# A hybrid decoder layer on one core: attention keys copied out of PSUM at once, the query statistic five half chunks behind its fold, softmax heads two half chunks apart

## The chip, the core and the metric

The kernel runs on one core of a Trainium2 chip. The metric is the device time of one execution in microseconds (us). The median of three executions of the kernel before is 1896.22 us (1896.04 to 1896.8). One further execution was recorded by the hardware profiler; its own time was 1896.41 us and its recorded span 1894.2 us. All rows shown below are of that execution.

## The reference

One decoder layer over 256 tokens of width 2048, float32 throughout. Three residual branches follow each other; each is normed on its way in and again on its way out:

```python
h = rms_norm(x, mix_pre_norm);   x = x + rms_norm(hybrid_mixer(h, ...), mix_post_norm)
h = rms_norm(x, xattn_pre_norm); m = rms_norm(mem, mem_norm)
x = x + rms_norm(cross_attention(h, m, wq, wkv, wo), xattn_post_norm)
h = rms_norm(x, ffn_pre_norm);   x = x + rms_norm(conv_glu_ffn(h, ...), ffn_post_norm)
```

The change lies in the second branch, the attention of 256 tokens over 256 memory tokens with 4 heads of 128:

```python
q = (h @ wq);  k, v = split(mem_n @ wkv)
p = softmax(einsum('bshd,bmhd->bhsm', q, k) * 128 ** -0.5)
return einsum('bhsm,bmhd->bshd', p, v) @ wo
```

## The kernel before

**Products.** Every weight matrix is cut into blocks of up to 512 columns, and each block into chunks of 512 KB that hold two slices of 128 rows (two values of `k`). A chunk is loaded by a DMA on SP's queue into one of four `raw` buffers. ACT casts it to `wh` (line 375) and DVE subtracts to get the rest, `wl` (line 396); each has four buffers. The left operand is split in the same way (`mh, ml` for the memory tokens, `qh, ql` for the normed residual), and TensorE (PE) multiplies three pairs: high by high, low by high, high by low. One slice `k` of a block is therefore 12 matmuls, a *half chunk*. Blocks of kind "fm" give outputs with features on partitions, "tm" with tokens on partitions. `acc` has four PSUM buffers and a block takes two, so the block after next cannot begin before somebody has read the block's results out (its *evacuation*).

**Order of work.** The program writes each engine's instructions in one fixed order. The function `run` goes through the blocks, half chunk by half chunk, and at each half chunk calls `side.half()`. That lets side tasks (Python generators: evacuations, norms, softmax) emit their next piece, up to their `yield`, between the products. Evacuations are bulk tasks, which wait for their turn by a budget of DVE and ACT time; a chain task (`chain=1`) emits one piece at every half chunk. `side.need(task)` emits all that is left of a task on the spot. So the place of a `yield` sets how many half chunks of products lie on PE between two pieces of a task.

**The attention's blocks.** The order is: `w_xk` (keys, operand `mh, ml`), two chunks of `w_xv` (values), all eight chunks of `w_xq` (queries, operand `qh, ql`), the other six chunks of `w_xv`, then four blocks of `w_xo`. `w_xk` and `w_xq` use the same two PSUM buffers. Three side works run beside them:

- `kx_evac`: DVE reads the key products out of PSUM into `kT`, scaled by the memory norm; a bulk task.
- `Residual.run`: DVE and ACT scale the mixer's output `z`, add it to the residual `xr`, and split it into `qh, ql`. The squares of `xr` are summed into `stx`. When all is summed, `early_column` folds the two halves of `stx` (DVE), and `column` then sums over partitions with two matmuls into `st`; from `st` come `var` (DVE) and the scale `stx_c` (GpSimd), which the softmax needs.
- `stagger` and `softmax`: per head, scores `xsc` (PE), row maximum `mx` (DVE), exponentials into `spr` (ACT), division (DVE, `psum` then `spr`), four transposes `xpT` (PE), copy to `pT` (ACT). `spr` has two halves that the heads use in turn. At the end `xo` (PE) multiplies the values `xv` by `pT`, and `split` (ACT, DVE) turns that into `oT`, the operand of the `w_xo` blocks.

The instructions of `act`, `dve` and the matmuls of `mm` are issued through helpers, so many rows of the profile carry line 66 (DVE and ACT) or 181 (PE); the tiles' names tell them apart.

Of the kernel before, what the change touches and what calls it, by code (L numbers as in the profile page):

```python
# [139 lines left out]
def layer(tc, d, dbg=None):  # L140
    with ExitStack() as ctx:
        ctx.enter_context(tc.manual_schedule())
        _layer(ctx, tc, tc.nc, d, dbg or (lambda n, t: None))


def _layer(ctx, tc, nc, d, dbg):
# [21 lines left out]
    def C(name, tag, shape=None, dt=F32):  # L168
        return mp.tile(shape or [P, S], dt, tag=tag, bufs=1, name=name)

    def small(name, shape, bufs=2):
        return mp.tile(shape, F32, tag="sm_" + name, bufs=bufs, name=name)
# [4 lines left out]
    def aux(name, shape=None):  # L177
        return pp.tile(shape or [P, 512], F32, tag="aux", bufs=4, name=name)

    def mm(out, lhsT, rhs, start=True, stop=True):  # L180
        pe.matmul(out, lhsT, rhs, start=start, stop=stop, skip_group_check=True)  # L181
# [61 lines left out]
    class Stat:  # L243
# [64 lines left out]

        def early_column(self):
            self.fold()  # L310
            yield
            yield
            self.column()

        def finish(self, n=2):
# [8 lines left out]
    def block(kind, srcs, xs, evac, before=None, cols=512, pool_=None, pre=None, bankwise=False, tail=0):  # L324

        blocks.append(dict(kind=kind, srcs=srcs, xs=xs, evac=evac, before=before, cols=cols,
                           pool=pool_ or acc, pre=pre, task=None, bankwise=bankwise, tail=tail))
        return blocks[-1]
# [103 lines left out]
    def run():  # L432
# [8 lines left out]
        for b, c0, c1 in order:  # L441
            if c0 == 0:
# [4 lines left out]
                n = (b["cols"] // P + 1) // 2 if b["kind"] == "fm" else 2 * (b["cols"] // 512)  # L447
# [57 lines left out]
            if nt:  # L505
# [9 lines left out]
                n = len(steps)  # L515
# [27 lines left out]
                feed.dma(i + 4)  # L543
            if end:
                b["task"] = side.add(b["evac"](banks))
                if b is xq_:
                    side.need(b["task"])
                pend.append(b["task"])

    def W(name, blk):  # L550
        return [d[name][blk, c] for c in range(d[name].shape[1])]
# [958 lines left out]
    for i in range(2):  # L1510
        for cb in range(4 + AHEAD):
            if cb >= AHEAD:
                before = None
                if cb == AHEAD:
                    before = need_hb if i else need_ha
# [15 lines left out]
    for b in range(4):  # L1531
        block("fm", W("w_mo", b), mo_xs, y_evac(b, sty, "z1", "postg"),
              before=load_x if b == 1 else None)
# [3 lines left out]
    mxs = lambda k: (M["mh"][:, k], M["ml"][:, k])  # L1537
# [13 lines left out]
    def qx_evac(ps):  # L1551
        M["qT"] = [T2("qT") for _ in range(2)]
        for g in range(2):
            act.copy(M["qT"][g], ps[g])
        tasks["sm"] = side.add(stagger([softmax(h) for h in range(4)]), chain=1, free=True)
        yield
# [10 lines left out]
    def stagger(gens):  # L1567

        live, left = [], list(gens)
        live.append(left.pop(0))  # L1570
        next(live[0])
        yield
        yield from M["res"].wait(4)
        while live or left:
            if left:
                live.append(left.pop(0))
            for g in list(live):
                try:
                    next(g)
                except StopIteration:  # L1580
                    live.remove(g)
            yield

    def softmax(h):
        qT, kT = M["qT"], M["kT"]
        q = aux("xsc", [P, 2, S])
        for t in range(2):
            mm(q[:, t], qT[h // 2][:, h % 2, t * P:(t + 1) * P], kT[h // 2][:, h % 2])
        mx = small("mx", [P, 2], bufs=4)
        dve.tensor_reduce(mx, q, axis=AX.X, op=ALU.max)  # L1590
        yield
        if h == 0:
            yield from M["res"].wait(4)
            M["spr"] = C("spr", "bg1", [P, 2, 2, S])
            M["sx"] = small("sx", [P, 2, 2], bufs=1)
            for i, sc in enumerate((128 ** -0.5, -128 ** -0.5)):
                dve.tensor_scalar(M["sx"][:, i], stx.rc, sc, None, op0=ALU.mult)
        sx = M["sx"]
        dve.tensor_mul(mx, mx, sx[:, 1])
        pr = M["spr"][:, h % 2]  # L1600
        ps_ = small("psum", [P, 2])
        for t in range(2):
            act.activation(pr[:, t], q[:, t], AF.Exp, scale=sx[:, 0, t:t + 1], bias=mx[:, t:t + 1], accum_out=ps_[:, t:t + 1])
        dve.reciprocal(ps_, ps_)
        for t in range(2):
            dve.tensor_scalar(pr[:, t], pr[:, t], ps_[:, t:t + 1], None, op0=ALU.mult)
        yield
        q = aux("xpT", [P, 2, S])
        for t in range(2):
            for mt in range(2):  # L1610
                pe.transpose(q[:, mt, t * P:(t + 1) * P], pr[:, t, mt * P:(mt + 1) * P], ident)
        if h % 2 == 0:
            M["pTs", h // 2] = C("pT", f"au{h // 2}", [P, 2, 2, S])
        M["pT", h] = M["pTs", h // 2][:, h % 2]
        act.copy(M["pT", h], q)
        yield
# [9 lines left out]
            split(M["oT"][:, 0, h2 * 2:h2 * 2 + 2], M["oT"][:, 1, h2 * 2:h2 * 2 + 2], q)  # L1626
            yield

    block("fm", W("w_xk", 0), mxs, kx_evac, before=start_res1)
    xv = block("tm", W("w_xv", 0), mxs, vx_evac, tail=2)  # L1630
    xq_ = block("fm", W("w_xq", 0), lambda k: M["res"].tile(k), qx_evac)
    st3 = Stat("st3")
# [6 lines left out]
    for b in range(4):  # L1639
        xo3 = block("fm", W("w_xo", b), lambda k: (M["oT"][:, 0, k], M["oT"][:, 1, k]), y_evac(b, st3, "z2", "xpostg"),  # L1640
              before=need_o if b == 0 else None, bankwise=b == 3)
# [67 lines left out]
    for b in range(32):  # L1709
        fu = block("fm", W("w_fu", b), fu_xs(b), fu_evac(b),  # L1710
              before=start_ffn if b == 0 else None, pool_=aux if b == 2 else acc)
# [126 lines left out]
    for n in range(2):  # L1838
        block("tm", W("w_fd", n), ax(n), fd_evac(n), cols=1024, pool_=acc if n else aux,
              tail=4 if n else 0)  # L1840
    run()
    drain_bulk()

# [91 lines left out]
```

## Time and profile before

| | |
|---|---|
| median of three runs | 1896.22 us |
| the profiled execution, its own time | 1896.41 us |
| its span | 1894.2 us |
| PE busy | 1878.4 us, 99% |
| DVE busy | 1297.0 us, 68% |
| ACT busy | 1012.7 us, 53% |
| `w_xk` ends, first chunks of `w_xv` begin | 744.8 us |
| first product of `w_xq` | 752.26 us |
| first scores | 777.68 us |
| first and last group of transposes | 782.96 and 793.21 us |
| `xo` begins | 803.74 us |

A row of a timeline gives the start in us, the duration, the engine, line, operation and tiles, a count where like instructions are merged, and in square brackets how long the engine sat idle before it and whose work ended that.

### The profile page before, as it was taken

To read this page: it belongs to the slowest core of one execution; us is meant where nothing else is said; L and a number is where in the kernel's file an instruction comes from. 1 tells how busy PE (TensorE), PEld (TensorE's weight loads), DVE (VectorE), ACT (ScalarE), POOL (GpSimd) and SP (SyncE) were. 2 spreads that over 40 slices of the span, in tenths; PEclk is the share of its full clock that TensorE was granted. 3 is DMA by queue.
4 is the path that set the end of the run, shared out by engine and by line. 5 is a ranking of instruction groups with operands and counts; after the bars stand their busy time and mean duration, and the time that the engine had idled before them with its cause. 6 is when DMAs were issued, how large, how long until landed. Compare 5 with 4: busy or idle time off the path is not lost.

```text
span 1894.2 us, 36440 instructions
## 1 busy us (share of the span) xinstructions
PE 1878.4 (99%) x15066; PEld 1788.5 (94%) x15066; DVE 1297.0 (68%) x1834; ACT 1012.7 (53%) x1467; POOL 22.4 (1%) x39
## 2 busy tenths in 40 slices
PE   9999999999999999899999999999999999999998
PEld 9999988999999999899999999999999998888886
DVE  7878787565675857677767766667766675556555
ACT  7676435555454645566555444455444455455554
POOL 0100000000000000000000000000000000000000
PEclk9999999999999999999999999999999999999999
DMA  7655554444556755455555555555566556556554
GB/s 267 184 168 182 183 157 149 136 153 157 167 171 210 268 201 179 134 163 186 193 189 190 191 198 193 197 190 190 191 198 196 195 190 219 192 190 198 191 191 142
DMA packets 98199, 352.20 MB, mean 186 GB/s; under 512 B 11057, under 2 KB 11825, under 8 KB 97649
## 3 DMA queue, kind: packets, MB, share of 16 engines
q1 hardware_dynamic: 97168, 348.86, 56.1%
q8 instruction: 118, 1.93, 0.4%
q10 hardware_dynamic: 864, 1.01, 0.2%
q14 instruction: 49, 0.39, 0.1%
HBM read 347.73 MB, written 2.10 MB: 185 GB/s over the span
## 4 chain that ended last, share of the span: by engine, by line
PE 95%; DVE 2%; ACT 1%; issue 1%; DMA 0%; ACTq 0%; DVEq 0%
PE fm L181 67%; PE tm L181 24%; DVE wl L396 1%; PE gram L181 0%; PE Y L181 0%; ACT wh L375 0%; DVE rows L66 0%; PE lv L181 0%; PE num L181 0%; DMA wsm<-in_w_sm_dram 0%; ACT spr L66 0%; PE X L181 0%; PE gramA L181 0%; PE U L181 0%; DVE ql L66 0%
## 5 line engine op out<-in xcount | busy, mean ns | idle before, releaser
L396 DVE TENSOR_TENSOR wl<-raw,wh 128x1024 fp32r<-128x1024 f32 x640 | 780.1, 1224 | 437.9 <-ACT wh L375 435.1
L375 ACT CAST wh<-raw 128x1024 fp32r<-128x1024 f32 x640 | 668.4, 1049 | 530.5 <-PE fm L181 408.6
L181 PE MATMUL fm<-fh,wh 128*128 128x256 f32 x2048 | 567.4, 277 | 1.4 <-ACT fh L66 1.4
L181 PE MATMUL fm<-fh,wl 128*128 128x256 f32 x2048 | 566.5, 277 | 0.0
L181 PE MATMUL fm<-fl,wh 128*128 128x256 f32 x2048 | 566.4, 277 | 0.0
L181 PEld LDWEIGHTS fm<-fh,wh 128*128 128x128 f32 x2048 | 384.9, 188 | 1.5 <-ACT fh L66 1.5
L181 PEld LDWEIGHTS fm<-fh,wl 128*128 128x128 f32 x2048 | 384.9, 188 | 0.0
L181 PEld LDWEIGHTS fm<-fl,wh 128*128 128x128 f32 x2048 | 384.9, 188 | 0.0
L181 PE MATMUL tm<-wh,as 128*128 128x512 f32 x1024 | 315.7, 390 | 0.8 <-DVE as L66 0.8
L181 PE MATMUL fm<-hh,wh 128*128 128x256 f32 x1072 | 301.9, 282 | 0.0
L181 PE MATMUL fm<-hh,wl 128*128 128x256 f32 x1072 | 299.7, 280 | 0.5 <-DVE wl L396 0.5
L181 PE MATMUL fm<-hl,wh 128*128 128x256 f32 x1072 | 299.3, 279 | 0.0
L181 PEld LDWEIGHTS tm<-wh,as 128*128 128x128 f32 x1024 | 192.2, 188 | 41.1 <-DVE as L66 1.1
L181 PEld LDWEIGHTS fm<-hh,wh 128*128 128x128 f32 x1072 | 202.8, 189 | 1.6 <-ACT hh L66 0.3
L181 PEld LDWEIGHTS fm<-hh,wl 128*128 128x128 f32 x1072 | 202.3, 189 | 1.2 <-DVE wl L396 0.9
L181 PEld LDWEIGHTS fm<-hl,wh 128*128 128x128 f32 x1072 | 202.3, 189 | 0.1
L181 PE MATMUL tm<-wl,as 128*128 128x512 f32 x512 | 199.3, 389 | 0.0
L181 PEld LDWEIGHTS tm<-wl,as 128*128 128x128 f32 x512 | 96.1, 188 | 19.9
L66 ACT CAST as<-ac 128x256 fp32r<-128x256 f32 x128 | 45.6, 405 | 110.8 <-PE tm L181 110.8
L66 DVE TENSOR_TENSOR as<-ac,as 128x256 fp32r<-128x256 f32 x128 | 48.6, 422 | 61.6 <-ACT as L66 61.6
L181 PE MATMUL fm<-mgh,wh 128*128 128x256 f32 x256 | 71.4, 279 | 0.0
L181 PE MATMUL fm<-mgl,wh 128*128 128x256 f32 x256 | 71.2, 278 | 0.0
(376 smaller groups left out, 2168.4 us busy)
## 6 DMA issues: line engine op xcount, KB each, us to landing
raw<-in_w_fu_dram SPq DMA_DIRECT2D x256, 512.0 KB, 4.3
raw<-in_w_in_dram SPq DMA_DIRECT2D x160, 512.0 KB, 3.7
raw<-in_w_fd_dram SPq DMA_DIRECT2D x128, 512.0 KB, 4.3
raw<-in_w_br_dram SPq DMA_DIRECT2D x32, 512.0 KB, 4.2
raw<-in_w_mo_dram SPq DMA_DIRECT2D x32, 512.0 KB, 4.3
raw<-in_w_xk_dram SPq DMA_DIRECT2D x8, 512.0 KB, 4.3
raw<-in_w_xv_dram SPq DMA_DIRECT2D x8, 512.0 KB, 3.7
raw<-in_w_xq_dram SPq DMA_DIRECT2D x8, 512.0 KB, 3.8
```

The lines of the kernel that those rows point to most:

```text
L66: return f(out, *a, **k)
L181: pe.matmul(out, lhsT, rhs, start=start, stop=stop, skip_group_check=True)
L375: nc.scalar.copy(wh, r)
L396: nc.vector.tensor_sub(wl, r, self.st[self.nl][0])
```

## The change

The work itself stays: the same products, the same copies, the same softmax. Four places set a new order:

- after the last half chunk of `w_xk`, its evacuation is emitted on the spot (`side.need`), where it had been left to the budget;
- `early_column` lets five half chunks pass between the fold of `stx` and the matmuls of `st`, where it had been two;
- `stagger` starts a new head at every second half chunk, where it had been every one;
- in `softmax`, two half chunks lie between the scores and the exponentials (they had been one), and three between the division and the transposes (one).

```diff
         def early_column(self):
             self.fold()
-            yield
-            yield
+            for _ in range(5):
+                yield
             self.column()
...
             if end:
                 b["task"] = side.add(b["evac"](banks))
-                if b is xq_:
+                if b is xq_ or b is xk:
                     side.need(b["task"])
                 pend.append(b["task"])
...
         yield from M["res"].wait(4)
+        n = 1
         while live or left:
-            if left:
+            if left and n % 2 == 0:
                 live.append(left.pop(0))
+            n += 1
             for g in list(live):
...
         dve.tensor_reduce(mx, q, axis=AX.X, op=ALU.max)
+        yield
         yield
         if h == 0:
...
         for t in range(2):
             dve.tensor_scalar(pr[:, t], pr[:, t], ps_[:, t:t + 1], None, op0=ALU.mult)
-        yield
+        for _ in range(3):
+            yield
         q = aux("xpT", [P, 2, S])
...
-    block("fm", W("w_xk", 0), mxs, kx_evac, before=start_res1)
+    xk = block("fm", W("w_xk", 0), mxs, kx_evac, before=start_res1)
```

What this does to the engines' orders, at three places. A minus marks a row at its place before, a plus at its place now. First DVE, where `w_xk` has ended:

```order
 L66 SCALAR_TENSOR_TENSOR ql<-xr_7893,par,qh 128x256 x2
 L66 TENSOR_TENSOR stx<-stx,sq 128x512
+L396 TENSOR_TENSOR wl<-raw,wh 128x1024
+L66 TENSOR_TENSOR kT<-fm,stm_b 128x512 x2
 L396 TENSOR_TENSOR wl<-raw,wh 128x1024 x2
 L66 TENSOR_TENSOR z_7900<-z_7900,stb 128x512
@@ -586,6 +588,4 @@
 L66 SCALAR_TENSOR_TENSOR ql<-xr_7893,par,qh 128x256 x2
 L66 TENSOR_TENSOR stx<-stx,sq 128x512
-L396 TENSOR_TENSOR wl<-raw,wh 128x1024
-L66 TENSOR_TENSOR kT<-fm,stm_b 128x512 x2
 L396 TENSOR_TENSOR wl<-raw,wh 128x1024 x2
```

The two copies to `kT` move up past two `wl`, a `z`, an `xr`, two `ql` and one `stx` addition, and the `wl` that stood right in front of them now stands in front of that `z`.

Second PE near the end of `w_xq`; of two pieces, the first is the old place of the statistic `st`, the second its new one:

```order
 L181 MATMUL fm<-ql,wh 128x256
 L181 MATMUL fm<-qh,wl 128x256
-L181 MATMUL st<-ones,stx 128x1 x2
 L181 MATMUL fm<-qh,wh 128x256
 L181 MATMUL fm<-ql,wh 128x256
```

```order
 L181 MATMUL fm<-ql,wh 128x256
 L181 MATMUL fm<-qh,wl 128x256
+L181 MATMUL st<-ones,stx 128x1 x2
 L181 MATMUL xsc<-kT,qT 128x256 x2
+L181 MATMUL tm<-wh,mh 128x256
```

The two matmuls move past 36 products, the last three half chunks of `w_xq`, and now stand directly in front of the first head's scores.

Third ACT at the end of the softmax and the beginning of `xo`:

```order
 L66 ACTIVATE spr,psum<-xsc,mx,sx 128x256 x2
 L66 COPY pT<-xpT 128x512
-L66 ACTIVATE spr,psum<-xsc,mx,sx 128x256 x2
-L375 CAST wh<-raw 128x1024
+L375 CAST wh<-raw 128x1024
+L66 ACTIVATE xv<-tm,stm_c 128x256 x2
 L66 COPY pT<-xpT 128x512
-L375 CAST wh<-raw 128x1024 x2
-L66 ACTIVATE xv<-tm,stm_c 128x256 x4
+L66 ACTIVATE xv<-tm,stm_c 128x256 x2
 L66 CAST oT<-xo 128x512 x2
```

The last copy to `pT` had two casts and all four `xv` activations behind it; it now stands between the two halves of `xv`. On PE the last head's transposes had 84 products between them and `xo`; now they stand directly in front of `xo`, and the four groups of transposes lie 60, 24, 36 and 24 products apart (counted from the first scores, with the other heads' scores between) where it had been 24, 12, 12 and 12.

## Prediction

> **What bounds the kernel now.** I read the page first, then the table of waits of PE, then the timelines of PE, DVE and ACT around the attention.
>
> ```profile
> span 1894.2 us, 36440 instructions
> PE 1878.4 (99%) x15066; PEld 1788.5 (94%) x15066; DVE 1297.0 (68%) x1834; ACT 1012.7 (53%) x1467; POOL 22.4 (1%) x39
> PEclk9999999999999999999999999999999999999999
> ```
>
> PE is busy for 99% of the span at full clock. No PE work is added or removed, so the change can win only PE's idle time, and lose only by making new idle time. The table of waits of PE says where that idle time is (total, times, longest):
>
> ```profile
> PE xpT L1611 <- DVE spr L66: 2.7, 4, 1.0
> PE st L181 <- DVE stx L66: 2.3, 1, 2.3
> PE fm L181 <- DVE kT L66: 1.6, 1, 1.6
> PE fm L181 <- ACT fh L66: 1.4, 1, 1.4
> ```
>
> Three of the four largest are the places that the change touches: 1.55 + 2.29 + 2.71 = 6.55 us, where the single values are in the brackets below. The fourth is the next branch's norm, which the change does not touch. PE's timeline at the three places, in the order of time, with the product in front of each stall:
>
> ```profile
> 750.43 0.28 PE L181 MATMUL tm<-wl,mh 128*128 128x256 f32 x1
> 752.26 0.36 PE L181 MATMUL fm<-qh,wh 128*128 128x256 f32 x1 [1.55 <-DVE kT L66]
> 752.46 0.28 PE L181 MATMUL fm<-ql,wh 128*128 128x256 f32 x1
> 752.58 0.28 PE L181 MATMUL fm<-qh,wl 128*128 128x256 f32 x1
> ...
> 770.17 0.28 PE L181 MATMUL fm<-qh,wl 128*128 128x256 f32 x1
> 772.74 0.61 PE L181 MATMUL st<-ones,stx 128*128 128x1 f32 x4 [2.29 <-DVE stx L66]
> 773.21 0.37 PE L181 MATMUL fm<-qh,wh 128*128 128x256 f32 x1
> 773.41 0.28 PE L181 MATMUL fm<-ql,wh 128*128 128x256 f32 x1
> ...
> 777.44 0.28 PE L181 MATMUL fm<-qh,wl 128*128 128x256 f32 x1
> 777.68 1.13 PE L181 MATMUL xsc<-kT,qT 128*128 128x256 f32 x4
> ...
> 782.96 0.70 PE L1611 MATMUL xpT<-con,spr 128*128 128x128 f32 x4 [0.43 <-DVE spr L66]
> ...
> 786.17 0.63 PE L1611 MATMUL xpT<-con,spr 128*128 128x128 f32 x4 [0.22 <-DVE spr L66]
> ...
> 790.12 0.63 PE L1611 MATMUL xpT<-con,spr 128*128 128x128 f32 x4 [1.02 <-DVE spr L66]
> ...
> 793.21 0.63 PE L1611 MATMUL xpT<-con,spr 128*128 128x128 f32 x4 [1.04 <-DVE spr L66]
> ...
> 803.74 3.62 PE L181 MATMUL xo<-pT,xv 128*128 128x256 f32 x16
> ```
>
> A product lasts 0.28 us, but the next starts 0.12 us after it (752.46 to 752.58). So a stall costs its bracket and 0.28 - 0.12 = 0.16 us more, in which PE is still counted busy; from start to start the first is 752.26 - 750.43 = 1.83 us, 1.71 over the pitch, and 1.55 + 0.16 is the same. The first product after it is 0.20 us long to the next start (752.26 to 752.46), 0.08 over the pitch. I cost stalls by starts, not by brackets.
>
> [...]
>
> **The first part: keys copied out at once.** The first product of `w_xq` needs the PSUM buffers of `w_xk`, which DVE empties into `kT`. DVE's timeline:
>
> ```profile
> 745.30 2.35 DVE L396 TENSOR_TENSOR wl<-raw,wh 128x1024 fp32r<-128x1024 f32 x2
> ...
> 751.43 1.29 DVE L66 TENSOR_TENSOR kT<-fm,stm_b 128x512 f32<-128x512 f32 x2
> 752.62 1.22 DVE L396 TENSOR_TENSOR wl<-raw,wh 128x1024 fp32r<-128x1024 f32 x1
> 756.24 1.23 DVE L396 TENSOR_TENSOR wl<-raw,wh 128x1024 fp32r<-128x1024 f32 x1 [2.39 <-ACT wh L375]
> ```
>
> and ACT's, the cast that ended this idle time:
>
> ```profile
> 755.15 1.05 ACT L375 CAST wh<-raw 128x1024 fp32r<-128x1024 f32 x1 [3.43 <-PE fm L181]
> ```
>
> In the new order `kT` follows the first `wl` of the first row: it starts at 745.30 + 1.14 = 746.44 and is done by 747.65 (two of 0.60). `w_xk`'s last product started about 744.7 (the `w_xv` chunks of 48 products at 0.12 end at 750.43), so DVE does not wait for it, and nothing behind `kT` is held. What moves behind it is later by 1.2 us: two `wl`, a `z`, an `xr`, two `ql`, a `stx`. Their readers are slices 2 to 7 of `w_xq`, from 3 us after its start, and DVE has done the same set of work at the same time as before, 753.8 (752.62 + 1.14), with 2.39 us of idle time behind. So the first product comes right after the last of `w_xv`, at 750.55. Gain: 1.71 + 0.08 = **1.8 us**. No DMA is issued by the moved step; the `raw` buffers come free up to 1.2 us later, against that idle time.
>
> Does the rest follow? The cast at 755.15 waits for PE to have read the first chunk of `w_xq`. With PE 1.8 us earlier the next `wl` starts at 754.45, still after 753.8, so DVE's chain of the residual runs 1.8 us earlier too.
>
> **The second part: the statistic later.** DVE at the end of that chain:
>
> ```profile
> 768.94 0.88 DVE L66 SCALAR_TENSOR_TENSOR ql<-xr,par,qh 128x256 fp32r<-128x256 f32 x2
> 769.73 1.48 DVE L66 TENSOR_TENSOR stx<-stx,sq 128x512 f32<-128x512 f32 x2
> ...
> 772.27 0.42 DVE L66 TENSOR_TENSOR stx<-stx 128x256 f32<-128x256 f32 x1
> ...
> 773.74 0.16 DVE L66 TENSOR_SCALAR var<-st 128x2 f32<-128x2 f32 x1
> ```
>
> The fold (772.27 to 772.70) is what `st` waited for. Now PE passes that place at 770.17 + 0.12 - 1.8 = 768.5 and goes on with 36 products, 4.2 us at the mean of 0.117 from 773.41 to 777.44; `st` is due at 772.7. The fold is done at 772.70 - 1.8 = 770.9, or at 772.7 if DVE's chain did not move at all: no wait in the one case, below 0.1 us in the other. The products that now run without the pause need their `ql`: the last two slices start at 769.9 and 771.3, their `ql` were done at 769.8 even unmoved. Gain: 772.74 - 770.17 - 0.12 = 2.45, and the 0.08 of the restart (773.21 to 773.41). The scores stood 0.24 us behind the last product (777.44 to 777.68) for the copy of the queries; `st` now fills that: 0.12 more. Together **2.65 us**. What is late next is the scale behind `st`: `var`, then GpSimd, then the exponentials; `st` comes out 0.3 us before the first scores, no longer 4 us. It costs nothing as long as the maximum and a `wl` keep DVE longer than that. GpSimd's part stands in the view of the tile `stx_c` (shortest, median and longest, in ns):
>
> ```profile
> L226 POOL TENSOR_TENSOR stx_c<-var,mhalf x1: 696/696/696, 774.0 to 774.0; 128x2 f32<-128x2 f32 x1
> ```
>
> `var` and this need 774.0 + 0.7 - 773.74 = 1.0 us; from the start of the scores to the scale's reader lie 778.85 - 777.68 = 1.2 to `mx`, 0.7 for it and 1.1 for a `wl`: 3.0.
>
> **The third part: the heads further apart.** A head's chain from scores to divided rows, and its period, stand on DVE and ACT:
>
> ```profile
> 778.85 0.69 DVE L66 TENSOR_REDUCE mx<-xsc 128x2 f32<-128x512 f32 x1 [1.74 <-PE xsc L181]
> 782.55 0.62 DVE L66 TENSOR_SCALAR spr<-spr,psum 128x256 f32<-128x256 f32 x2
> 785.67 0.62 DVE L66 TENSOR_SCALAR spr<-spr,psum 128x256 f32<-128x256 f32 x2
> 789.62 0.62 DVE L66 TENSOR_SCALAR spr<-spr,psum 128x256 f32<-128x256 f32 x2
> 792.71 0.62 DVE L66 TENSOR_SCALAR spr<-spr,psum 128x256 f32<-128x256 f32 x2
> ```
>
> The first head's rows are ready 782.55 + 0.62 - 777.68 = 5.5 us after the scores start; the others follow 3.1 to 3.95 us apart, the longer where a `wl` (1.14) lies in between. Now each head has one, so I take 4.0. PE, from the first scores: 60 products of 0.12 and three groups of scores of 0.9 (1.03 to 1.13 less 0.16) to the first transposes, 9.9 us; then 24 products, a score group and 0.47 of transposes (0.63 less 0.16), 4.2; then 36 products and 0.47, 4.8; then 24 and 0.47, 3.3. So PE arrives at 9.9, 14.1, 18.9 and 22.2 us, and the rows are ready at 5.5, 9.5, 13.5 and 17.5: over 4 us to spare each time. The stalls go whole: brackets 0.43 + 0.22 + 1.02 + 1.04 = 2.71 and 4 x 0.16 = 0.64, **3.35 us**. The exponentials of heads 2 and 3 overwrite the halves of `spr` that the transposes of heads 0 and 1 read: PE frees them at 10.4 and 14.6, they are wanted about 2 us before the rows are ready, at 11.5 and 15.5.
>
> The end of this part is the tight place. The last copy to `pT` and the second half of `xv` had about 10 us of products in front of `xo`; now the transposes stand right there. On ACT:
>
> ```profile
> 793.87 0.59 ACT L66 COPY pT<-xpT 128x512 f32<-128x512 f32 x1 [0.46 <-PE xpT L1611]
> ...
> 803.93 0.84 ACT L66 ACTIVATE xv<-tm,stm_c 128x256 f32<-128x256 f32 x2 [1.98 <-PE tm L181]
> ```
>
> The copy starts 793.87 - 793.21 = 0.66 us after the transposes and takes 0.59, `xv` takes 0.84 behind it: done at 2.1 us. `xo`'s second half, which needs both, starts 0.47 + 3.62/2 = 2.3 us after the transposes. `xo`'s first half hides them with 0.2 us to spare; with that cover gone, ACT being late by 1 us costs 0.8.
>
> **The sum.** 1.8 + 2.65 + 3.35 = 7.8 us off the profiled execution's own 1896.41 gives 1888.6. The median of the runs is 0.2 below that execution, so I predict a median of **1888.4 us**, 0.41% less.
>
> **Rivals.** (a) *Brackets are the whole of it.* If PE only wins the idle time that the table counts, the gain is 6.55 and the median 1889.7. For it: it is the profile's own account; against it: the start-to-start gaps. (b) *DVE takes over in `w_xq`.* PE, PEld, DVE and ACT between `kT` and `st`, by the table of stretches:
>
> ```profile
> 752.30:772.70 20.40, 18.15 (x156) 17.94 (x156) 17.80 (x28) 12.11 (x19) 0.00 (x0) 1.00 0.46 155
> ```
>
> DVE is busy for 17.80 of 20.40 us, and 2.39 of the rest is the one gap before 756.24. If the residual's chain does not start earlier, PE gives the first 1.8 us back to a wait on `ql` or on the fold: 6.0 gained, 1890.2. Against it: the times above leave PE at most 0.1 us behind even then, unless ACT or the loads slip too. (c) *The softmax chain becomes PE's bound, slower than before.* The heads hang on one loop, DVE to ACT and back, once per head, with a cast on each engine now inside every turn. At the last head it has 22.2 - 17.5 = 4.7 us to spare over three turns; from a period of 4.0 + 4.7/3 = 5.6 us on, PE waits in front of the last transposes, and one large stall replaces the four. To eat the gain it needs 4.0 + (4.7 + 7.8)/3 = 8.2 us a turn; at 9.5 the stall is 11.8 us and the median 1896.2 + 4 = 1900. For it: strict order on both engines, and a cast that waits for a buffer holds the exponentials behind it. Against it: 8 us is twice the longest period in the rows above. (d) *The wait moves to `xo`:* ACT late by 1 to 2 us there, 0.8 to 1.8 given back, 1889.2 to 1890.2.
>
> **How the numbers follow.** The forecast 0.72, (a) 0.11, (b) 0.06, (d) 0.08, (c) 0.03. Differences under about 0.2% (3.8 us) can't be told from no change here. The forecast's own range is 1887.6 to 1889.2 (what the rows don't show: 0.3 us of restarts, 0.4 of scatter between runs). The range of 8 in 10 takes in (a), (d) and (b) and some scatter below: 1887.0 to 1890.9. Singly, all but (c) lie below 1892.4. I take 0.04 for several of them together reaching no change; of the 0.03 of (c), 0.01 ends there too: faster 0.93, same 0.05, slower 0.02.
>
> **What would show it.** In the new trace: no bracket on the first product of `w_xq`, which starts about 750.55 behind `kT` at 747.65; `st` without a bracket about 773, fold 2 us ahead; no bracket at any `xpT`; `xo` about 795.9 instead of 803.74; PE idle down by 6.5 us in the table. It is wrong if PE waits for `ql` or `wl` between 755 and 773, for `spr`, or if `xo` shows a wait on `pT` or `xv` over half a us.

## The result and the profile after

The changed kernel takes 1889.35 us (median of six runs, 1888.89 to 1889.73) against 1897.03 us for the kernel before (six runs, 1896.04 to 1898.68): a ratio of 0.9958, 95% interval 0.9946 to 0.9971, or 7.7 us less. Later both kernels were timed again: 1888.71 us (five runs) against 1897.94 (29 runs), ratio 0.9955, 0.9943 to 0.9967, 9.2 us less. The prediction was 1888.4, range 1887.0 to 1890.9. Of the runs told of below, two lie far off all others of their kernel (1927.0 us with the keys alone, 6688.43 us with two half chunks) and are left out of the medians and ratios.

The head of the page of the changed kernel, and its table of waits of PE:

```profile
span 1887.2 us, 36442 instructions
PE 1877.2 (99%) x15066; PEld 1788.2 (95%) x15066; DVE 1296.5 (69%) x1834; ACT 1012.3 (54%) x1467; POOL 22.4 (1%) x39
```

```profile
PE fm L181 <- ACT fh L66: 1.4, 1, 1.4
PE warm L181 <- POOL ones L210: 1.1, 1, 1.1
PE sum L181 <- ACT diag L66: 0.9, 1, 0.9
PE fm L181 <- DVE wl L396: 0.8, 2, 0.5
```

The three waits on `spr`, `stx` and `kT` are gone from the table, and the attention has no new one. Two short waits that the profile of before did not have (0.34 us at 7.00, 0.32 us at 56.55) lie at the start of the kernel, far ahead of the change. PE's timeline at the same places as before:

```profile
751.34 0.28 PE L181 MATMUL tm<-wl,mh 128*128 128x256 f32 x1
751.46 0.28 PE L181 MATMUL fm<-qh,wh 128*128 128x256 f32 x1
751.58 0.28 PE L181 MATMUL fm<-ql,wh 128*128 128x256 f32 x1
...
773.59 0.28 PE L181 MATMUL fm<-qh,wl 128*128 128x256 f32 x1
773.71 0.50 PE L181 MATMUL st<-ones,stx 128*128 128x1 f32 x4
774.07 1.11 PE L181 MATMUL xsc<-kT,qT 128*128 128x256 f32 x4
...
783.90 0.60 PE L1615 MATMUL xpT<-con,spr 128*128 128x128 f32 x4
...
788.06 0.60 PE L1615 MATMUL xpT<-con,spr 128*128 128x128 f32 x4
...
792.80 0.60 PE L1615 MATMUL xpT<-con,spr 128*128 128x128 f32 x4
...
796.10 0.60 PE L1615 MATMUL xpT<-con,spr 128*128 128x128 f32 x4
796.53 3.62 PE L181 MATMUL xo<-pT,xv 128*128 128x256 f32 x16
```

No row has a bracket, and PE goes from one block to the next at its pitch of 0.12 us. One number must be read with care: this execution came to the attention 0.9 us later than the profiled one of before (the first product of `w_xv` at 745.70, before 744.79), although nothing ahead of it was changed. In the 14 profiles of this study that moment lies between 743.9 and 745.7; it is scatter. The length from there to the first row of `xo` is free of it, and I use it below as *the stretch*: 803.74 - 744.79 = 58.95 us before, 796.53 - 745.70 = 50.83 us after, **8.1 us less**. Up to the first product of the next branch, at 833.32 before and at 826.29 after, 7.9 us of it are left.

### The profile page after: what moved, and what is told of

It reads as the page before. It is cut to its first block, busy times and chain, and to the rows that moved or that the text cites. A ratio compares the mean times of both kernels' runs of the same rounds, so it can differ in the third digit from the quotient of the medians.

```text
span 1887.2 us, 36442 instructions
## 1 busy us (share of the span) xinstructions
PE 1877.2 (99%) x15066; PEld 1788.2 (95%) x15066; DVE 1296.5 (69%) x1834; ACT 1012.3 (54%) x1467; POOL 22.4 (1%) x39
## 4 chain that ended last, share of the span: by engine, by line
PE 95%; DVE 2%; DMA 1%; ACT 1%; issue 0%; SPq 0%; ACTq 0%; DVEq 0%
PE fm L181 67%; PE tm L181 24%; DMA raw<-in_w_in_dram 1%; DVE wl L396 1%; DMA x<-in_x_dram 1%; PE gram L181 0%; ACT wh L375 0%; PE Y L181 0%; DVE rows L66 0%; PE lv L181 0%; PE num L181 0%; PE X L181 0%; PE gramA L181 0%; PE U L181 0%; PE zg L181 0%
```

## The experiments

All runs of one table row are timed beside the kernel before on the same chip; the last four rows come from another chip than the first eight. The stretch is that of the one profiled execution of each kernel; it ends where `xo` begins, so a wait inside `xo` is not in it.

| kernel | median us (before) | ratio, 95% interval | stretch us |
|---|---|---|---|
| keys alone | 1895.92 (1897.94) | 0.9994, 0.9985 to 1.0003 | 58.78 |
| statistic alone | 1893.81 (1897.94) | 0.9982, 0.9974 to 0.9991 | 55.80 |
| heads alone | 1895.10 (1897.94) | 0.9987, 0.9978 to 0.9995 | 56.90 |
| all three | 1888.71 (1897.94) | 0.9955, 0.9943 to 0.9967 | 50.83 |
| all, one half chunk behind the fold | 1895.13 (1898.03) | 0.9985, 0.9977 to 0.9994 | 57.68 |
| all, two half chunks | 1892.99 (1898.03) | 0.9972, 0.9962 to 0.9983 | 55.16 |
| all, three half chunks | 1890.35 (1898.03) | 0.9961, 0.9948 to 0.9975 | 52.21 |
| all, transposes not later | 1888.87 (1898.03) | 0.9954, 0.9942 to 0.9967 | 50.82 |
| all, two multiplications more a head | 1889.04 (one run) | | 50.83 |
| all, four multiplications more | 1890.93 (1898.37) | 0.9962, 0.9947 to 0.9977 | 52.86 |
| all, three copies more before `xv` | 1888.84 (one run) | | 50.84 |
| transposes later, heads not spaced | 1893.60 (1898.37) | 0.9974, 0.9964 to 0.9984 | 55.49 |

### The three parts alone

The theory was that each stall is worth its gap from start to start, and that DVE's chain of the residual follows PE. The rivals were the brackets as the whole gain, and DVE taking over. The edits are the three groups of lines of the diff, one at a time:

```diff
# keys alone
-                if b is xq_:
+                if b is xq_ or b is xk:
# statistic alone, in early_column
-            yield
-            yield
+            for _ in range(5):
+                yield
# heads alone: the edits in stagger and softmax
```

> Only the keys' early copy out of PSUM, the rest as before. Theory (each stall is worth its gap from start to start, and DVE's chain of the residual follows PE): the bracket of 1.55 us on the first product of w_xq goes, the stall in front of st stays as it was (2.3 us), the transposes' too (2.7 us); 1.8 us less than before. Rival (DVE takes over): DVE's chain does not start earlier, the stall in front of st grows to 2.3 + 1.8 = 4.1 us, and the time is that of before within 0.3 us. Rival (brackets): 1.55 us less.

> Only the query statistic five half chunks behind its fold, the rest as before. Theory: no bracket at st, the stall at the first product of w_xq stays 1.55 and those of the transposes 2.7; 2.65 us less than before. Rival (brackets): 2.3 us less. Rival (the wait moves on): the scale behind st comes too late for the first exponentials and the first transposes' stall grows by 1 us or more, so 1.6 us less or below.

> Only the softmax's three edits (a head every second half chunk, two half chunks to the exponentials, three to the transposes), the rest as before. Theory: no bracket at any transposes, none at xo; the other two stalls stay 1.55 and 2.3; 3.35 us less than before. Rival (brackets): 2.7 us less. Rival (the wait moves to xo): a bracket on xo of 0.8 us or more, 2.5 us less or below.

> The whole change again, beside its parts. Theory: the parts add up, 7.8 us less than before, within 0.5 us of the sum of the three parts alone. Rival (parts share a gain or give it back): the whole falls short of the sum of its parts by 1 us or more.

By the waits in the attention, each part does what it should and nothing else: its own bracket goes, the others stay within 0.05 us, but for 1.24 in place of 1.55 us on `kT` with the statistic alone. The stall in front of `st` did not grow with the keys alone, so DVE did follow PE and that rival falls. But the keys alone brought the stretch down by 0.2 us only, with 1.8 expected, and the interval of its timed ratio holds 1. With the heads alone it came down by 2.05 us, with 3.35 expected. PE's timeline of the keys alone shows where the rest went:

```profile
768.12 0.28 PE L181 MATMUL fm<-qh,wl 128*128 128x256 f32 x1
770.66 0.61 PE L181 MATMUL st<-ones,stx 128*128 128x1 f32 x4 [2.26 <-DVE stx L66]
771.13 0.46 PE L181 MATMUL fm<-qh,wh 128*128 128x256 f32 x1
771.39 0.42 PE L181 MATMUL fm<-ql,wh 128*128 128x256 f32 x1
771.61 0.41 PE L181 MATMUL fm<-qh,wl 128*128 128x256 f32 x1
```

Behind the stall the products start 0.21 us apart, not 0.12. The tables of stretches from `st` to the first scores (length; busy time of PE, PEld, DVE, ACT, POOL; granted clock; DMA) give the cause. First before the change, then the keys alone, then the heads alone:

```profile
772.70:777.70 5.00, 4.96 (x41) 4.79 (x41) 2.42 (x3) 1.63 (x2) 0.70 (x1) 1.00 0.69 210
```

```profile
770.60:777.10 6.50, 6.44 (x41) 6.24 (x41) 2.44 (x4) 1.64 (x2) 0.70 (x1) 0.74 0.54 164
```

```profile
773.30:779.80 6.50, 6.45 (x41) 6.26 (x41) 2.42 (x3) 1.64 (x2) 0.70 (x1) 0.74 0.67 191
```

The same 41 rows take 6.50 us in place of 5.00, at a mean granted clock of 0.74. By PE's rows the products start 0.21 us apart from 771.39 to 774.59 with the keys alone and from 775.00 to 778.21 with the heads alone, about 3.4 us with the first and the last slow gap, and 0.12 apart behind that. A mean of 0.74 over 6.50 us is then 1.00 for 3.1 us and 0.50 for the 3.4: the clock was half for 2 x 0.26 x 6.5 = 3.4 us. PE's own stall, 2.54 and 2.58 us from start to start, had been followed by a half clock in these two executions; in the one profiled before the change a stall of 2.57 us had not (1.00 in the first table). Without these 1.5 us the stretch is 57.3 with the keys alone and 55.4 with the heads alone; with the statistic alone it is 55.8, and 0.3 us of that gain belong to the shorter wait on `kT`:

| part | expected | stretch, clock and `kT` set even | median of the runs |
|---|---|---|---|
| keys | 1.8 | 1.65 | 2.0 |
| statistic | 2.65 | 2.85 | 4.1 |
| heads | 3.35 | 3.55 | 2.8 |
| sum | 7.8 | 8.05 | 9.0 |
| all three | 7.8 | 8.1 | 9.2 |

The parts add up. The statistic and the heads lie well above their brackets (2.29 and 2.71), the keys between bracket and forecast (1.55 and 1.8). By the sum, 8.1 against 6.55, the rival of the brackets falls. In the timed runs the statistic is worth more than its stall.

### How long a stall halves the clock

The theory was formed from those rows: a stall in front of `st` of some 2.5 us brings the clock to half for 3.4 us in a part of the executions (two of three profiles so far). That a longer one does so always was the author's guess; no run had shown it. The rival was that the stall costs its own length. The edit sets the length of the stall, in the whole change, by the half chunks between fold and statistic:

```diff
             self.fold()
-            for _ in range(5):
+            for _ in range(1):     # then 2, then 3
                 yield
```

> The whole change, but one half chunk between the fold and the statistic instead of five. The fold ends when it did, so PE stands still in front of st for about 3.9 us. New theory (a stall of some 2.5 us or more can bring PE's clock to half for 3.4 us): that slow stretch comes in every run, behind the stall; 4.0 us for the stall and 1.5 to 1.7 for the slow products more than the whole change, about 1894.4, with little scatter. Rival (the stall alone): 4.0 us more, about 1892.7, and a granted clock of 1.00 in the stretch behind st.

> The whole change, but two half chunks between the fold and the statistic, as before the change: keys and heads alone. The stall in front of st is 2.3 us by its bracket. New theory (clock): two groups of runs 1.5 us apart, about 1891.4 and 1892.9, the slower one with half the clock behind st. Rival (the stall alone): one group about 1891.4, with the scatter of the whole change (1 us from lowest to highest).

> The whole change, but three half chunks between the fold and the statistic. Both theories: the stall in front of st is 1.0 us by its bracket; the clock stays whole and the runs lie close together, 1.1 to 1.4 us above the whole change, about 1890.0. If the clock falls even here, there are two groups.

The stretches behind the stall, with three, two and one half chunks:

```profile
771.70:775.30 3.60, 3.51 (x29) 3.32 (x29) 2.37 (x4) 0.82 (x3) 1.61 (x1) 1.00 0.71 209
```

```profile
771.20:777.70 6.50, 6.47 (x41) 6.27 (x41) 2.41 (x3) 1.64 (x3) 0.70 (x1) 0.74 0.49 164
```

```profile
771.00:780.00 9.00, 8.96 (x53) 8.77 (x53) 2.56 (x3) 1.64 (x2) 1.65 (x1) 0.67 0.37 117
```

and the stalls that lead to them, in the same order:

```profile
770.68 0.28 PE L181 MATMUL fm<-qh,wl 128*128 128x256 f32 x1
771.79 0.61 PE L181 MATMUL st<-ones,stx 128*128 128x1 f32 x4 [0.82 <-DVE stx L66]
```

```profile
768.69 0.28 PE L181 MATMUL fm<-qh,wl 128*128 128x256 f32 x1
771.23 0.61 PE L181 MATMUL st<-ones,stx 128*128 128x1 f32 x4 [2.26 <-DVE stx L66]
```

```profile
767.05 0.28 PE L181 MATMUL fm<-qh,wl 128*128 128x256 f32 x1
771.04 1.01 PE L181 MATMUL st<-ones,stx 128*128 128x1 f32 x4 [3.71 <-DVE stx L66]
```

With 1.1 us from start to start the clock stays whole (1.00 in the first table), and the five runs lie within 0.8 us (1889.81 to 1890.57); they are 1.6 us above the whole change by the median and 1.4 by the stretch (1.1 to 1.4 expected). With 2.5 us the runs fall in two groups, 1891.4 and 1891.8 against 1892.9 to 1893.1 (five); the profiled one, of the second group, has the 0.74. They lie 2.9 and 4.3 us above the whole change: the stall alone, and the stall with 1.5 us. With 4.0 us the mean of 0.67 makes 2 x 0.33 x 9.0 = 5.9 us at half clock behind the start of `st`, longer than the 3.4 expected. It was low from there on: `st` takes 0.87 us to the next start (771.04 to 771.91), where it takes 0.47 behind the stall of 2.5 us (771.23 to 771.70). When it fell, the rows do not show. The median is 6.4 us above the whole change (5.5 to 5.7 expected). The cost varies there too: 1893.3 to 1896.4. The rival falls.

This also tells of the kernel before, whose stall at `st` is 2.57 us: its 47 runs beside these two groups of experiments spread from 1895.5 to 1899.8, the whole change's eleven from 1888.5 to 1889.7. The mean granted clock of whole runs is on record, rounded to 0.001, and 3.4 us at half clock lower it by 0.0009. Of all 60 runs of the kernel before that were timed beside the experiments, 29 stand at 0.998 (median 1898.5 us), 29 at 0.999 (1897.5) and two at 1.000. At 0.998 stand also nine of eleven runs of the heads alone and four of eleven of the keys alone, which keep the stall, and one of eleven of the statistic alone, which removes it; that one is its slowest (1897.15). The 27 runs of the whole change and of its variants with no gap above 2.2 us in the attention never stand below 0.999. This fits a half clock in a part of the runs of the kernel before, one that makes up some of their spread (1898.5 against 1897.5 us). The mean does not say where in a run the clock fell, so how much of the spread it is stays open.

### What the heads need

Two edits take the softmax's three apart:

```diff
# transposes not later (the other two as changed)
-        for _ in range(3):
-            yield
+        yield
# transposes later, heads not spaced: the three half chunks alone
-            if left and n % 2 == 0:
+            if left:
...
         dve.tensor_reduce(mx, q, axis=AX.X, op=ALU.max)
-        yield
         yield
```

> The whole change, but one half chunk between the division and the transposes, as before: a head every second half chunk and two to the exponentials remain, and 24 products lie between the last transposes and xo. Theory (what counts is that PE comes to each transposes later than the rows, which follow 4 us apart): PE arrives at 6.1, 10.3, 14.5 and 19.3 us after the first scores, the rows are ready at 5.5, 9.5, 13.5 and 17.5, so no stall and the time of the whole change within 0.4 us. Rival (the later transposes carry the gain): brackets at the transposes of 0.5 us or more each, 2 to 3 us above the whole change.

> The keys and the statistic as changed; of the softmax's edits only the three half chunks between division and transposes, with a new head at every half chunk and one to the exponentials as before. Theory: the four scores and 48 products bring PE to the first transposes at 9.3 us, then every 1.9 us (11.2, 13.1, 15.0); the rows are ready at 5.5, 8.6, 12.5 and 15.6 with one wl inside the loop: at most 0.6 us of stall in front of the last, 0 to 0.6 us above the change. Rival (heads must be spaced): a stall of 1.5 us or more at the third and fourth transposes.

Without the later transposes nothing is lost: no bracket, the stretch is 50.82, the time 1888.87. So one of the edits is not needed: a head every second half chunk, with two half chunks in front of the exponentials, already brings PE to each group of transposes after its rows. Which of these two is needed was not tried. The second kernel does not compute the same: with a new head at every half chunk, the exponentials of heads 2 and 3 are written into the two halves of `spr` before heads 0 and 1 are transposed, so these two are transposed with the others' rows. That order also makes the first transposes wait for head 2, which my expectation had left out:

```profile
786.15 0.94 PE L1612 MATMUL xpT<-con,spr 128*128 128x128 f32 x4 [2.87 <-DVE spr L66]
```

```profile
786.10:791.50 5.40, 5.35 (x32) 5.21 (x33) 2.93 (x7) 3.21 (x7) 0.00 (x0) 0.68 0.10 41
```

The clock was low again, 0.68 over 5.40 us, behind a gap of 3.1 us from start to start (2.87 of bracket and the 0.28 of the product before it). So the stall that the rival foretold came, but from the two halves of `spr` and not from the pace of the loop, and the run says nothing on that.

### The rooms: the loop of DVE and ACT, and the cover in front of `xo`

The prediction gave the softmax chain 4.7 us of room at the last head, and the end of the chain 0.2 us in front of `xo`'s second half. Both were tried by adding work:

```diff
         dve.reciprocal(ps_, ps_)
+        for _ in range(2):          # then 4
+            nc.vector.tensor_scalar(pr, pr, 1.0, None, op0=ALU.mult)
...
         act.copy(M["pT", h], q)
+        for _ in range(3 if h == 3 else 0):
+            nc.scalar.copy(M["pT", h], q)
```

> The whole change, and on DVE two multiplications of a head's rows by 1.0 more in each head, between the reciprocal and the division (0.53 us each, 1.07 a turn). In the trace of the change the last head's rows were ready 4.6 us before PE came to its transposes. Theory: four turns use 4.3 of the 4.6 us; no bracket over 0.3 us at the transposes, none at xo, the time of the change. Rival (DVE has no such room, every us on it counts): 4 us more.

> As the run before with four multiplications in each head, 2.13 us a turn, a period of 6.1 us. Theory: 8.5 us in four turns less 4.6 us of room is 3.9 us of stalls at the transposes, the first none, the later ones growing; 3.9 us above the change, still below the kernel before. If the loop of DVE and ACT is not what decides, the stall is near nothing, or the whole 8.5 us.

> The whole change, and the last head's copy to pT done three times more on ACT (0.48 us each, 1.44 in all), in front of the second half of xv. Theory: the second half of xv is done 2.1 + 1.44 = 3.5 us after the start of the last transposes, the second half of xo is due at 2.3; PE waits 1.2 to 1.3 us inside xo. Rival (xo has more room than 0.2 us): no wait.

With two multiplications a head there is no bracket and no loss. With four, DVE and PE show:

```profile
778.21 1.79 DVE L1609 TENSOR_SCALAR spr<-spr 128x512 f32<-128x512 f32 x4
780.04 0.62 DVE L66 TENSOR_SCALAR spr<-spr,psum 128x256 f32<-128x256 f32 x2
...
785.70 0.62 DVE L66 TENSOR_SCALAR spr<-spr,psum 128x256 f32<-128x256 f32 x2
```

```profile
797.51 0.63 PE L1617 MATMUL xpT<-con,spr 128*128 128x128 f32 x4 [1.84 <-DVE spr L66]
```

A turn is 5.66 us (780.04 to 785.70), so one multiplication adds (5.66 - 3.95) / 4 = 0.43 us to it, not 0.53 (the time of the two halves of a division in the whole change, 778.91 to 779.44), and four turns add 4 x 1.7 = 6.8. Less the 4.6 us of room that leaves 2.2; from start to start the one stall is 1.84 + 0.28 = 2.12, or 2.0 over the pitch, and the stretch is 2.0 us longer. The loop decides as the prediction put it, its room is right, and only the size of my added work was off. The time, 1890.93, is 1.9 us above the single run with two multiplications on the same chip. The gap of 2.1 us did not lower the clock: the transposes behind it take 0.47 us to the next start (797.51 to 797.98), where they took 0.59 behind the gap of 3.1 us (786.15 to 786.74), and the mean clock of each of the four runs is 0.999 or 1.000.

With three copies more on ACT, in front of `xv`'s second half, PE and ACT show:

```profile
794.33 0.60 PE L1615 MATMUL xpT<-con,spr 128*128 128x128 f32 x4
794.77 1.89 PE L181 MATMUL xo<-pT,xv 128*128 128x256 f32 x8
797.84 1.99 PE L181 MATMUL xo<-pT,xv 128*128 128x256 f32 x8 [1.18 <-ACT xv L66]
799.48 0.59 PE L181 MATMUL fm<-oT,wh 128*128 128x256 f32 x2
```

```profile
794.97 0.59 ACT L66 COPY pT<-xpT 128x512 f32<-128x512 f32 x1 [1.02 <-PE xpT L1615]
795.59 1.82 ACT L1621 COPY pT<-xpT 128x512 f32<-128x512 f32 x3
797.30 0.85 ACT L66 ACTIVATE xv<-tm,stm_c 128x256 f32<-128x256 f32 x2
```

and ACT in the whole change:

```profile
796.74 0.58 ACT L66 COPY pT<-xpT 128x512 f32<-128x512 f32 x1 [1.03 <-PE xpT L1615]
797.22 0.84 ACT L66 ACTIVATE xv<-tm,stm_c 128x256 f32<-128x256 f32 x2
```

PE waits 1.18 us inside `xo` by the bracket, which is what was expected (1.2 to 1.3), but that agreement is luck. By starts, from the transposes to the first product of `w_xo`, it takes 799.48 - 794.33 = 5.15 us, where the whole change takes 799.80 - 796.10 = 3.70: 1.45 us are lost. And `xv` starts 797.30 - 794.97 = 2.33 us behind the first copy, where it had been 0.48: the copies made it 1.85 us later, not 1.44. So the room in front of `xo`'s second half is 1.85 - 1.45 = 0.4 us, not the 0.2 that the prediction took from the rows; PE goes on 0.54 us after `xv` has started, before its record ends at 798.15. Beyond that room a delay of ACT here does cost PE. The median of one run does not show it above the scatter; the rows do.

## Why the prediction was right, and where it was short

**Keys.** In the new trace `kT` is done 3 us ahead of its reader, and DVE keeps 0.63 us of idle time behind it:

```profile
747.34 1.28 DVE L66 TENSOR_TENSOR kT<-fm,stm_b 128x512 f32<-128x512 f32 x2
...
755.45 1.23 DVE L396 TENSOR_TENSOR wl<-raw,wh 128x1024 fp32r<-128x1024 f32 x1 [0.63 <-ACT wh L375]
```

Less the scatter of 0.9 these are 746.4 and 754.55; the prediction had 746.44 and 754.45, and 0.65 of idle time. The first product, 751.46, is the predicted 750.55 plus 0.9.

**Statistic.** The fold ends at 771.9 and `st` starts at 773.71, 1.8 us of room as predicted. The scale behind it was no new wait: DVE waits for the scores, not for GpSimd.

```profile
771.48 0.42 DVE L66 TENSOR_TENSOR stx<-stx 128x256 f32<-128x256 f32 x1
...
775.21 0.69 DVE L66 TENSOR_REDUCE mx<-xsc 128x2 f32<-128x512 f32 x1 [0.74 <-PE xsc L181]
...
776.95 0.23 DVE L66 TENSOR_SCALAR sx<-stx_c 128x2 f32<-128x2 f32 x2
```

**Heads.** The rows of a head follow 3.95 to 4.02 us apart where 4.0 was predicted, and the transposes come 4.4 us or more after them (the first at 783.90, with its rows ready at 779.53):

```profile
778.91 0.62 DVE L66 TENSOR_SCALAR spr<-spr,psum 128x256 f32<-128x256 f32 x2
...
782.86 0.62 DVE L66 TENSOR_SCALAR spr<-spr,psum 128x256 f32<-128x256 f32 x2
...
786.88 0.62 DVE L66 TENSOR_SCALAR spr<-spr,psum 128x256 f32<-128x256 f32 x2
...
790.90 0.62 DVE L66 TENSOR_SCALAR spr<-spr,psum 128x256 f32<-128x256 f32 x2
```

By starts in the two profiles the three parts are worth 1.8, 2.7 and 3.6 us, where 1.8, 2.65 and 3.35 were predicted. Of the rivals, the brackets (a) fall by the stretch, 8.1 against 6.55; DVE taking over (b) and the wait at `xo` (d) did not come. The loop (c) is real, with its point at 5.6 us a turn found where it was put: at 5.66 and a first turn that is later by as much, the wait is 2 us.

**What failed** is a sentence at the head of the prediction: "PE is busy for 99% of the span at full clock ... so the change can win only PE's idle time". It held for the one execution that was profiled (1.00 behind `st`). In the profiles of the keys alone and of the heads alone the same stall is followed by a half clock (0.74 over 6.50 us), which is no idle time and stands in no table of waits; the mean clocks of 0.998 fit that it came in runs of the kernel before too. The second part was therefore mis-sized for the timed runs: 2.65 us predicted, 4.1 measured, of which the trace explains 2.85 by starts; the half clock costs 1.5 us (6.50 against 5.00) in the profiles in which it comes. That is a likely reason, not a shown one, why the gain came out larger in the second set of runs, 9.2 us after 7.7, while the changed kernel moved by 0.6 us only: the clock of the first set's runs of the kernel before is not on record. That the forecast of the median came so close is in part luck: the three runs that it started from (median 1896.22) lie at the low end of those of the kernel before (1895.5 to 1899.9). From 1897.94 the same sum gives 1890.1, still inside the range. The row of the clock that I read is that of one execution; a single profile cannot show what comes in a part of the runs. A smaller term was off too: the room in front of `xo`'s second half, put at 0.2 us, is 0.4.

## What to carry to other kernels

Count a stall of PE from the start of one product to the start of the next, less the pitch: the bracket leaves out what PE is still counted busy for, here 0.16 us a stall, about 1 us of the 8.1 over six stalls. When spacing a chain that crosses engines, work out when the consumer arrives and when the row is ready for each turn, and find the smallest room; for the loop of DVE and ACT it told within 0.2 us what added work would cost (2.2 worked out, 2.0 measured). Check such a room by starts too: in front of `xo` a bracket agreed with an expectation whose two halves were both off. And a stall of PE can cost more than itself: one of 2.5 us from start to start cost 1.5 us more in three of four profiles here. Runs that scatter more than the kernel's other versions do are a reason to look at the granted clock behind the longest stall.

## What the hardware showed beyond the expected

A gap of 2.5 us between two starts on PE was followed by a half clock in three profiled executions of this study (keys alone, heads alone, two half chunks: 0.74 over 6.50 us each) and by a whole one in one, the kernel before (1.00 over 5.00 us). In the three the products started 0.21 us apart in place of 0.12, for about 3.4 us, which cost 1.5 us. The clock did not fall in the gap itself: by the starts in PE's rows it fell about 0.6, 1.5 and 0.7 us after PE had begun again. Gaps of 1.1, 1.8 and 2.1 us (three half chunks and `kT` before, both 1.00 in the stretch behind; four multiplications, whose profiled run has a mean of 1.000) were followed by no fall in the one profile of each. Behind one of 3.1 us (0.68 over 5.40 us) there were about 2 x 0.32 x 5.4 = 3.5 us of half clock, behind one of 4.0 us (0.67 over 9.00 us) 5.9 us, both low from PE's first row on. What decides at 2.5 us was not tried.
